# Where the tiles of a four-layer block lie in SBUF: weights at 448, halves and other 2 KB tiles at 128 modulo 512 bytes

## The chip, the core and the metric

The kernel runs on one NeuronCore of a Trainium2 chip. The metric is the device time of one execution, in microseconds: the median of the timed runs of the kernel before is 1500.3 us (1500.19 to 1500.99, three runs). The profiled execution, from which all rows come, took 1500.85 us.

## The reference

Two blocks follow one another on x of 256 positions by 1,024 features, all in float32. Cut to what matters for the work on the chip:

```python
def first_block(x, ...):                       # two layers
    for l in range(2):
        h = rms_norm(x, norm_mix[l])
        x = x + (pool_attn_mixer if l % 2 == 0 else rglru_mixer)(h, ...)
        h = rms_norm(x, norm_ffn[l])
        x = x + conv_ffn(h, ...)               # 1024 -> 2 x 2816 -> 1024

def hybrid_layer(x, pe, ...):                  # two layers of the second block
    proj = rms_norm(x, g_mix) @ w_in           # queries, keys, values, 3 x 1024 gates
    merged = (gates[0] * (o_mla @ w_branch[0]) + gates[1] * (o_diff @ w_branch[1])
              + gates[2] * (o_win @ w_branch[2]))
    x = x + merged @ w_out
    h = rms_norm(x, g_ffn)
    a = depthwise_conv(h @ w_ffn_gate, conv_w, conv_b)
    x = x + (gelu(a) * (h @ w_ffn_up)) @ w_ffn_down
    return x + sigmoid(rms_norm(x, g_ple_in) @ w_ple_gate) * rms_norm(pe @ w_ple_proj, g_ple)
```

Nearly all the arithmetic is products of x (or of something as wide) with weight matrices that are used once.

## The kernel before

The weights come from memory as one stream of chunks, each up to 128 partitions by 2,048 float32 (8 KB in a partition). `_push` (line 247) loads a chunk into `st`, ScalarE rounds it to `hi` (a float32r copy, line 262), and VectorE writes what the rounding lost to `lo` (line 263). There are three buffers of each, and two chunks are prepared ahead. Activations are kept as two halves in the same way: `xx` holds the normalised x transposed (both halves side by side, written at lines 391 and 392), `o` the outputs of the attention heads, `hg` the products inside the feed-forward nets, `w4` some others.

A product of two such pairs is three matmuls, `mm3` (line 277): high by high, high by low, low by high. TensorE multiplies a stationary operand (128 columns, loaded by a LDWEIGHTS of its own before every matmul) with a moving one of 256 to 512 columns. Two forms alternate:

- feature-major (`fm_pair`, `fm_first`, `fm_wide`, `gate`, `branch`): the weights are stationary, and the halves of x or of the attention move, 256 columns at a time (512 at line 608, where both halves of `xx` move at once);
- token-major (`tm_block`, `tm_wide`): the halves are stationary, and the weights move, 512 columns at a time.

```python
    def mm3(self, out, ah, al, bh, bl, start, stop):
        mm = self.pe.matmul
        mm(out, ah, bh, start=start, stop=False)
        mm(out, ah, bl, start=False, stop=False)
        mm(out, al, bh, start=False, stop=stop)
```

In a group of the profile `T<-xx,hi` means: written to PSUM tile `T`, moving operand `xx`, stationary operand `hi`; the first name behind the arrow is the moving one. Matmuls that go through the in-order wrapper show line 207.

The order of the work is set by a scheduler that the framework runs over the program as it is written; matmuls of the merge stage keep the written order. All weight chunks are issued on SyncE's queue.

A tile is asked for by a tag with `t` (line 227). All tiles of a tag share its buffers (`SB`, line 225, says how many), and a tag's buffers get their place in SBUF when it is asked for the first time, one tag behind the other in that order. So the order of first requests sets every address. A partition's row of a chunk, of `xx`, `o` and `hg` is cut in steps of multiples of 512 bytes: k blocks, halves and column blocks all start at the tile's own address modulo 512, except in one chunk of 416 columns for each hybrid layer.

Of the kernel before, what the change touches and what calls it, by code (L numbers as in the profile page):

```python
# [19 lines left out]
P = 128  # L20
S = 256
D = 1024
# [7 lines left out]
CHUNK = 2048  # L30
# [179 lines left out]
class Net:  # L210
# [66 lines left out]
# [5 lines that stand above are left out]
# [165 lines left out]
    def start(self):  # L447
        nc, ap = self.nc, self.ap
        self.vecs = self.t(list(ap["vec"].shape), "vec")
        self.ident = self.t([P, P], "ident")  # L450
        g0 = self.vat["gain0"]
        self.act_o.dma_start(self.ident, ap["ident"])
        self.act_o.dma_start(self.vecs[:, g0:g0 + KD], ap["vec"][:, g0:g0 + KD])
        self.x = self.t([P, 2, D], "x")
        self.sync_o.dma_start(self.x[:, 0, :], ap["x"][:P, :])
        for _ in range(3):
            self._push()
        self.rows = self.t(list(ap["row"].shape), "row")
        self.ones = self.t([P, P], "ones")
        self.sync_o.dma_start(self.vecs[:, g0 + KD:], ap["vec"][:, g0 + KD:])  # L460
        self.sync_o.dma_start(self.ones, ap["ones"])
        self.sync_o.dma_start(self.rows, ap["row"])
        self.acc = None
# [443 lines left out]
    def chained(self, mms):  # L907

        last = None
        for out, lhsT, rhs, start, stop in mms:  # L910
            ins = self.pe.matmul(out, lhsT, rhs, start=start, stop=stop)
            if last is not None:
                self.after(ins, [last])
            last = ins
# [506 lines left out]
```

## Time and profile before

| | |
|---|---|
| median of the runs | 1500.3 us (1500.19 to 1500.99) |
| profiled execution | 1500.85 us, its span 1499.0 us |
| PE (matmul) busy | 1486.7 us, 99% of the span |
| PEld (weight load) busy | 1328.7 us, 89% |
| DVE busy | 1160.4 us, 77% |
| ACT busy | 935.2 us, 62% |
| POOL busy | 108.0 us, 7% |
| DMA | 257.29 MB, 172 GB/s on average |

The busy time of PE is the union of its matmuls, which overlap; it says that one was always under way, not at which rate they follow one another. The rate is read from starts in the timeline, divided by the count between them.

### The profile page before, as it was taken

What the parts mean: (1) busy time and instruction counts of PE and PEld (TensorE: products, weight loads), DVE (VectorE), ACT (ScalarE), POOL (GpSimd) and SP (SyncE); (2) the same over time, 40 slices, a digit from 0 to 9 for tenths busy, and PEclk for the clock granted to TensorE, in tenths of its full rate; (3) what the DMA queues carried; (4) which work ended last, traced back from release to release, by engine and by line L of the source; (5) the groups of instructions that cost most, each with busy time, mean ns of one, the idle gap of its engine ahead of it and who ended that gap; (6) DMA issues with size and microseconds to landing.
All of it is one profiled execution on the core that took longest, in us unless ns stands there. A gap on an engine that the chain in (4) does not pass through costs nothing.

```text
span 1499.0 us, 24541 instructions
## 1 busy us (share of the span) xinstructions
PE 1486.7 (99%) x9540; PEld 1328.7 (89%) x9540; DVE 1160.4 (77%) x2257; ACT 935.2 (62%) x1684; POOL 108.0 (7%) x101
## 2 busy tenths in 40 slices
PE   8999999999999999999999999999999999999998
PEld 6789999999999998899988988888899998988896
DVE  6669777789797777885877877778886877877766
ACT  7757555586666556765765755656766664765554
POOL 0200000000000000012530000000003250000000
PEclk9999999999999999999999999999999999999999
DMA  7455455444454554543335455544443334555551
GB/s 285 160 190 197 170 197 193 165 148 169 158 208 171 195 175 159 197 169 113 136 119 190 171 206 186 197 169 167 168 183 126 130 125 169 190 197 178 190 194 56
DMA packets 37877, 257.29 MB, mean 172 GB/s; under 512 B 4385, under 2 KB 4769, under 8 KB 8321
## 3 DMA queue, kind: packets, MB, share of 16 engines
q1 hardware_dynamic: 36576, 252.38, 47.5%
q0 software_dynamic: 896, 3.28, 0.6%
q8 instruction: 75, 1.23, 0.3%
q14 instruction: 42, 0.34, 0.1%
q10 hardware_dynamic: 288, 0.07, 0.0%
HBM read 254.66 MB, written 1.05 MB: 171 GB/s over the span
## 4 chain that ended last, share of the span: by engine, by line
PE 95%; DVE 3%; issue 1%; ACT 1%; DMA 0%; SPq 0%; ACTq 0%
PE A L207 14%; PE A L279 10%; PE A L280 10%; PE A L281 10%; PE S L281 4%; PE S L280 4%; PE S L279 4%; PE T L281 4%; PE T L280 4%; PE T L279 4%; PE S L608 4%; PE T L608 4%; PE T L207 2%; PE S L207 2%; PE O L279 2%; PE O L280 2%
## 5 line engine op out<-in xcount | busy, mean ns | idle before, releaser
L263 DVE TENSOR_TENSOR lo<-st,hi 128x1024 fp32r<-128x1024 f32 (+3 forms) x480 | 574.2, 1210 | 143.1 <-ACT hi L262 142.1
L262 ACT ACTIVATE hi<-st 128x1024 fp32r<-128x1024 f32 (+3 forms) x480 | 490.0, 1043 | 245.3 <-PE A L207 65.6
L207 PE MATMUL A<-xx,hi 128*128 128x256 f32 x768 | 142.5, 287 | 0.0
L281 PE MATMUL S<-xx,lo 128*128 128x256 f32 x496 | 141.4, 285 | 0.0
L280 PE MATMUL S<-xx,hi 128*128 128x256 f32 x496 | 140.8, 284 | 0.0
L279 PE MATMUL S<-xx,hi 128*128 128x256 f32 x496 | 140.1, 283 | 0.0
L281 PE MATMUL T<-xx,lo 128*128 128x256 f32 x480 | 136.4, 284 | 0.0
L280 PE MATMUL T<-xx,hi 128*128 128x256 f32 x480 | 136.3, 284 | 0.0
L279 PE MATMUL T<-xx,hi 128*128 128x256 f32 x480 | 136.2, 284 | 0.0
L207 PEld LDWEIGHTS A<-xx,hi 128*128 128x128 f32 x768 | 118.2, 189 | 8.2 <-issue 7.9
L279 PE MATMUL A<-hi,xx 128*128 128x512 f32 (+2 forms) x304 | 117.1, 387 | 0.2 <-ACT xx L391 0.2
L280 PE MATMUL A<-lo,xx 128*128 128x512 f32 (+2 forms) x304 | 116.2, 382 | 0.0
L281 PE MATMUL A<-hi,xx 128*128 128x512 f32 (+2 forms) x304 | 115.9, 383 | 0.0
L281 PE MATMUL A<-hi,hg 128*128 128x512 f32 x294 | 115.1, 391 | 0.6 <-DVE hg L314 0.6
L279 PE MATMUL A<-hi,hg 128*128 128x512 f32 x294 | 115.6, 393 | 0.0
L280 PE MATMUL A<-lo,hg 128*128 128x512 f32 x294 | 115.4, 393 | 0.0
L207 PE MATMUL A<-xx,lo 128*128 128x256 f32 x384 | 108.3, 282 | 0.0
L1113 POOL TENSOR_SCALAR s<-s,at 128x256 f32<-128x256 f32 x56 | 56.4, 1024 | 577.5 <-DVE at L958 577.0
L279 PEld LDWEIGHTS S<-xx,hi 128*128 128x128 f32 x496 | 94.1, 190 | 0.1
L281 PEld LDWEIGHTS S<-xx,lo 128*128 128x128 f32 x496 | 93.8, 189 | 0.1
L280 PEld LDWEIGHTS S<-xx,hi 128*128 128x128 f32 x496 | 93.6, 189 | 0.1
L279 PEld LDWEIGHTS T<-xx,hi 128*128 128x128 f32 x480 | 91.1, 190 | 0.9
(377 smaller groups left out, 3464.2 us busy)
## 6 DMA issues: line engine op xcount, KB each, us to landing
st<-in_w_dram SPq DMA_DIRECT2D x230, 1024.0 KB, 4.8
st<-in_w_dram SPq DMA_DIRECT2D x4, 832.0 KB, 4.8
st<-in_w_dram SPq DMA_DIRECT2D x2, 768.0 KB, 4.2
x<-in_x_dram SPq DMA_DIRECT2D x2, 512.0 KB, 5.0
st<-in_w_dram SPq DMA_DIRECT2D x4, 256.0 KB, 6.5
st<-in_w_dram SPq DMA_DIRECT2D x2, 512.0 KB, 3.5
w<-in_gain_dram POOLq DMA_DIRECT2D x2, 512.0 KB, 4.0
out_dram<-x SPq DMA_DIRECT2D x4, 256.0 KB, 2.0
```

Source lines behind the costliest of these rows:

```text
L207: return lambda *a, **k: self.tc.keep_in_program_order(f(*a, **k))
L262: nc.scalar.activation(hi[:, c0:c1], st[:, c0:c1], AF.Copy)
L263: nc.vector.tensor_tensor(out=lo[:, c0:c1], in0=st[:, c0:c1], in1=hi[:, c0:c1].bitcast(F32), op=ALU.subtract)
L279: mm(out, ah, bh, start=start, stop=False)
L280: mm(out, ah, bl, start=False, stop=False)
L281: mm(out, al, bh, start=False, stop=stop)
L608: mm(banks[e], wh[:, k, c], self.xx[:, k, :], start=k == 0, stop=False)
L1113: nc.gpsimd.tensor_scalar(s[:, c], s[:, c], r[:, t:t + 1], None, op0=ALU.mult)
```

## The change

At the very start of the program, after `vec`, `ident` and `x`, one tile of each of 16 tags is asked for, in a chosen order, and never written. Nothing else is changed. The order, the number and the waits of the instructions on all five engines are the same in both programs, and so is the turn in which buffers of a tag are used; the lines behind move down by two.

```diff
         self.x = self.t([P, 2, D], "x")
+        for tag, n in (("st", CHUNK), ("hi", CHUNK), ("lo", CHUNK), ("ssx", 4), ("ess", 4), ("trcos", 32)) + (("xx", 4 * D), ("w4", D), ("o", D), ("hg", 512), ("w6", 1536), ("s", 512), ("pT", 512), ("qk", 512), ("w2", 512), ("bias", 512)):
+            self.t([P, n], tag)
         self.sync_o.dma_start(self.x[:, 0, :], ap["x"][:P, :])
```

The addresses in a partition that follow (first buffer of a tag, and what is left of it modulo 512), as the two programs place them:

| tag | holds | before | modulo 512 | after | modulo 512 |
|---|---|---|---|---|---|
| x, ident | x, identity | 19904, 19392 | 448 | the same | 448 |
| st, hi, lo | weight chunks | 28096, 52672, 77248 | 448 | the same | 448 |
| xx | halves of x, merged halves | 105024 | 64 | 102016 | 128 |
| w4 | projections, halves of the embedding | 131232 | 160 | 118400 | 128 |
| o | halves of the attention | 155808 | 160 | 142976 | 128 |
| hg | products of the nets, gates | 201344 | 128 | 159360 | 128 |
| w6 | queries, keys, merged sum | 189056 | 128 | 175744 | 128 |
| s | scores, net columns | 176288 | 160 | 188032 | 128 |
| pT | transposed probabilities, net columns | 184736 | 416 | 196224 | 128 |
| qk | transposed queries and keys, net columns | 172192 | 160 | 200320 | 128 |
| w2 | scratch | 121440 | 96 | 204416 | 128 |
| bias | position bias | 127136 | 160 | 208512 | 128 |
| ones | ones | 104512 | 64 | 215296 | 256 |
| rb | row scales | 217728 | 128 | 217888 | 288 |
| dist | distances | 218816 | 192 | 218976 | 352 |

The three small tags behind `lo` (`ssx`, `ess`, `trcos`) take 192 bytes, which lead from 448 to 128.

## Rows read from the trace of the kernel before

**Rows 1.** The page: TensorE's busy time, and the chain's shares by engine.
```profile
PE 1486.7 (99%) x9540; PEld 1328.7 (89%) x9540; DVE 1160.4 (77%) x2257; ACT 935.2 (62%) x1684; POOL 108.0 (7%) x101
...
PE 95%; DVE 3%; issue 1%; ACT 1%; DMA 0%; SPq 0%; ACTq 0%
```

**Rows 2.** Waits of PE: us in total, times, longest.
```profile
PE S L355 <- DMA ident<-in_ident_dram: 4.7, 1, 4.7
PE T L355 <- DMA x<-in_x_dram: 1.2, 1, 1.2
PE A L281 <- DVE hg L314: 0.6, 1, 0.6
PE A L279 <- ACT xx L391: 0.2, 1, 0.2
```

**Rows 3.** Windows: length, busy PE, PEld, DVE, ACT, POOL, clock, DMA share, GB/s.
```profile
243.60:260.63 17.03, 17.03 (x121) 16.03 (x120) 13.03 (x20) 9.50 (x15) 0.00 (x0) 1.00 0.53 188
854.18:870.93 16.75, 16.75 (x91) 14.36 (x90) 14.49 (x37) 9.87 (x16) 0.00 (x0) 1.00 0.55 194
```

**Rows 4.** Timeline of PE, one net unit: start, duration, group; first of each stream.
```profile
243.61 0.28 PE L279 MATMUL T<-xx,hi 128*128 128x256 f32 x1
...
255.12 0.39 PE L279 MATMUL A<-hi,hg 128*128 128x512 f32 x1
...
260.63 0.28 PE L279 MATMUL T<-xx,hi 128*128 128x256 f32 x1
```

**Rows 5.** Groups of PEld: count, busy us, mean ns.
```profile
L279 PEld LDWEIGHTS A<-hi,hg 128*128 128x128 f32 x294 | 55.3, 188 | 11.3
...
L207 PEld LDWEIGHTS A<-xx,hi 128*128 128x128 f32 x768 | 118.2, 189 | 8.2 <-issue 7.9
```

**Rows 6.** Timeline of PE, the product with w_out: its first, and the next's.
```profile
795.17 0.39 PE L279 MATMUL A<-hi,xx 128*128 128x512 f32 x1
...
817.47 0.49 PE L386 MATMUL S<-ident,x 128*128 128x128 f32 x3
```

**Rows 7.** Timeline of PE, 120 matmuls of the branches: first, and the next's.
```profile
1239.48 0.39 PE L207 MATMUL A<-o,hi 128*128 128x256 f32 x1
...
1253.78 0.39 PE L279 MATMUL A<-hi,xx 128*128 128x512 f32 x1
```

**Rows 8.** Timeline of PE, an earlier net unit's 96 matmuls.
```profile
141.58 0.28 PE L279 MATMUL T<-xx,hi 128*128 128x256 f32 x1
...
152.97 0.39 PE L279 MATMUL A<-hi,hg 128*128 128x512 f32 x1
```

**Rows 9.** Groups by form, halves stationary.
```profile
L279 PE MATMUL A<-hi,xx 128*128 128x512 f32 x240 | 96.5, 404 | 0.0
...
L281 PE MATMUL A<-hi,o 128*128 128x512 f32 x26 | 10.6, 406 | 0.0
...
L280 PE MATMUL T<-lo,xx 128*128 128x512 f32 x8 | 3.2, 395 | 0.0
```

**Rows 10.** Groups by form, halves moving.
```profile
L207 PE MATMUL A<-xx,hi 128*128 128x256 f32 x768 | 142.5, 287 | 0.0
...
L608 PE MATMUL S<-xx,hi 128*128 128x512 f32 x240 | 85.6, 394 | 0.0
...
L207 PE MATMUL A<-o,hi 128*128 128x256 f32 x256 | 47.3, 286 | 0.0
...
L281 PE MATMUL A<-xx,lo 128*128 128x256 f32 x112 | 31.3, 282 | 0.0
```

**Rows 11.** Timeline of PE, 32 wide pairs: the first, and the next stream's.
```profile
859.69 0.40 PE L608 MATMUL T<-xx,hi 128*128 128x512 f32 x1
...
870.92 0.40 PE L279 MATMUL A<-hi,hg 128*128 128x512 f32 x1
```

**Rows 12.** Groups by form of VectorE, the costliest.
```profile
L263 DVE TENSOR_TENSOR lo<-st,hi 128x1024 fp32r<-128x1024 f32 x460 | 557.1, 1224 | 131.6 <-ACT hi L262 130.7
```

## The prediction

> **What bounds the kernel now.** I read the engines' busy shares first, then the chain that ended last, then the waits, then the instruction groups, then single starts. The reader is to see that TensorE alone sets the time: its matmuls cover 99% of the span and the chain is 95% PE [rows 1]. All its waits that the profile names come to 6.7 us (4.7 + 1.2 + 0.6 + 0.2), most of it before the first matmul [rows 2]. So a buffer that comes free sooner, or a DMA that lands sooner, gives nothing; only a shorter step from one matmul to the next does. [...]
>
> The mean duration of a matmul in the groups (287 ns for 256 columns) is no price, since matmuls overlap. The price is the distance between starts. One unit of a feed-forward net before its wide form is 96 matmuls of 256 columns and 24 of 512. The 96 run from 243.61 to 255.12 us, 119.9 ns each; the 24 from 255.12 to 260.63 us, 229.6 ns each [rows 4]. [...] The weight loads take 188 to 189 ns each whatever tile they read [rows 5], and there is one for every matmul. [...]
>
> [...] Both of the following streams have 512 columns, moving from weight buffers at 448 modulo 512, with the same loop (`tm_wide`), and differ in where the stationary tile lies. With the nets' products (`hg`, at 128) it is 229.6 ns [rows 4]; with the merged halves in the x tile (`xx`, at 64), 96 matmuls from 795.17 to 817.47 us, 232.3 ns [rows 6]. So 128 is 2.7 ns better than 64 beside 448.
>
> For the moving operand there is one row only, and not of 128: 120 matmuls of 256 columns moving from `o` (at 160), with weights at 448 stationary, go from 1239.48 to 1253.78 us, 119.2 ns each [rows 7], against 119.9 for `xx` at 64. And the address isn't all: an earlier run of the same 96 matmuls at the same addresses takes 141.58 to 152.97 us, 118.6 ns each [rows 8]. Streams fall into one rhythm or another, 1.3 ns apart.
>
> [...]
>
> **The change part by part.** No instruction is added, removed or moved, on any queue, and no wait changes; tiles get other addresses. Weight buffers (`st`, `hi`, `lo`), `x` and `ident` keep theirs.
>
> 1. Stationary operand from 64 to 128, `xx` under 512 columns: 14 groups, of which the largest and the smallest are shown, 960 matmuls in all [rows 9]. At 2.7 ns: 2.6 us. All on the path, since PE waits for nothing between them.
> 2. Stationary operand from 160 to 128 (`o`, and the `w4` halves): 216 matmuls, the largest group of 26 shown [rows 9]. No clean stream of them stands in the trace; at the same 2.7 ns, 0.6 us. Bounds: nothing and twice that.
> 3. Moving operand from 64 to 128, `xx`, 256 columns: 13 groups, the largest and the smallest shown, 4,896 matmuls [rows 10]. This term decides, and its price is in no row. Upper end of the gain: what the stationary operand gives, 2.7 ns, if only the distance between the two operands counts: 13.2 us. Lower end: the same 2.7 ns lost, if the pair 128 moving, 448 stationary is a bad one; 13.2 us slower. The nearest row is `o` at 160, 0.7 ns better than 64, and the pair of 128 and 448 is the best that the trace shows, though with the roles exchanged. I take the middle of these two, 1.7 ns: 8.3 us.
> 4. Moving operand from 64 to 128, `xx`, 512 columns (L608): 480 matmuls [rows 10], at the same 1.7 ns: 0.8 us. With its partner of 256 columns such a pair takes 351 ns now (32 pairs from 859.69 to 870.92 us, [rows 11]).
> 5. Moving operand from 160 to 128 (`o` in the branches): 256 + 128 + 3 x 64 = 576 matmuls, the largest group shown [rows 10]. By terms 3 and the row of 160, 1.7 - 0.7 = 1.0 ns: 0.6 us; bounds 2 us either way.
> 6. VectorE, ScalarE and GpSimd tiles (`s`, `pT`, `qk`, `w2`, `bias` from 160, 416 or 96 to 128; `rb` from 128 to 288, `dist` from 192 to 352): I cost them at nothing. What hides them is TensorE: in the net's unit DVE is busy 13.03 us of 17.03 and ACT 9.50 [rows 3], so each could be 20% slower before it ended last. VectorE's largest group by far, 460 subtractions of 1,224 ns, reads `st` and `hi` and writes `lo`, none of which moves [rows 12]. Transposes read `ident` and their source in float32; they are few, and I leave them at nothing.
>
> Sum: 2.6 + 0.6 + 8.3 + 0.8 + 0.6 = 12.9 us of matmul steps. What is late next when they go? With 4 us of slack for DVE in a unit of 17 us that gets 0.15 us shorter, nothing; but a few waits behind norms don't shrink, so I count 12.5. The profiled execution took 1500.85 us (span 1499.0 and 1.85 around it), 0.5 above the median of 1500.3. 1500.85 - 12.5 = 1488.3, and against the median 1487.8. I say 1488.
>
> **The rivals.**
> *The weight load alone sees its address.* Then terms 1 and 2 stay and 3 to 5 vanish: 3.2 us, 1497.5. For it: the only clean pair of rows differs on the stationary side. Against it: `o` at 160 as moving operand is 0.7 ns faster than `xx` at 64, but that is less than the 1.3 ns between two rhythms of one address.
>
> *Nothing changes.* The difference between `hg` and `xx` comes from the rhythm or the position in the program, not from the address: 1500.5. For it: the two rhythms. Against it: 96 matmuls of `xx` and 24 of `hg` each keep their value where they recur. [...]
>
> *Slower: the distance has a sign.* In the stream of 229.6 ns the stationary operand lies 192 bytes past the moving one (128 - 448, modulo 512); in that of 232.3 ns it lies 128 past. After the change the 256-column matmuls have it 320 past (448 - 128), a distance no row shows; now it is 384. If 320 is a bad distance the 5,376 matmuls of terms 3 and 4 pay up to 2.7 ns, 14.5 us, less the 3.2 us won: 1500.5 + 11.3, about 1512. It decides from 0.6 ns a matmul on (3.2 / 5,376). For it: three in four of the matmuls whose operand moves are of this kind, and the trace has no row of that distance. Against it: 128, a multiple of 128 bytes, is the only placement in the trace that is better than the others.
>
> **How the numbers follow.** The forecast (both operands gain; its own range 1479 to 1493, from half the moving gain to 2.7 ns with the better rhythm's 1.3 ns on top) 0.52; the weight load alone 0.20; nothing 0.09; slower 0.19. About 0.2%, 3 us, can be told from no change. The second case, at 3.2 us, sits on that line: I give 0.13 of it to faster and 0.07 to same. Faster 0.65, same 0.16, slower 0.19. The range from 1478 to 1504 leaves out the far end of each side: the slow case beyond 1.2 ns a matmul, and gains above those two together.
>
> **What the profile after would show.** Right: the 96 matmuls of the net's unit below 118.6 ns a step, and `xx` under 512 columns at 229 to 230 ns, with `hg` unchanged at 229.6. Term 1 is wrong if the 96 of the merged halves still take 22.3 us. Term 3 is wrong if the unit's 96 still take 11.5 us, and the slow rival is right if they take over 11.6. Wrong for another reason: a wait of PE for DVE or ACT that grows beyond 1 us in sum, or busy times of VectorE's groups on `rb` or `s` that change by several per cent. The forecast as a whole fails if the step of the 256-column matmuls moves by less than 0.5 ns.

## The result, and the profile after

The changed kernel takes 1484.5 us (median of four runs, 1484.14 to 1485.4), against 1500.2 for the kernel before on the same chip (1499.89 to 1500.99): a ratio of 0.9895, 95% interval 0.9883 to 0.9907. The forecast was 1488.0, with a range of 1478 to 1504. The profiled execution took 1484.23 us, at a mean granted clock of 1.000 as before.

The page of the changed kernel, busy times and the chain's shares by engine:

```profile
span 1482.3 us, 24541 instructions
...
PE 1469.4 (99%) x9540; PEld 1312.3 (89%) x9540; DVE 1160.1 (78%) x2257; ACT 934.1 (63%) x1684; POOL 106.9 (7%) x101
...
PE 87%; DVE 8%; ACT 3%; issue 2%; DMA 0%; ACTq 0%
```

TensorE is busy for 17.3 us less, the other engines as long as before to within 1.1 us [rows 1]. More of the chain now passes through VectorE (8% against 3%), which invites the reading that PE waits for it. The waits of PE that the profile names (us in total, times, longest) say no; they are those of [rows 2]:

```profile
PE S L355 <- DMA ident<-in_ident_dram: 4.7, 1, 4.7
PE T L355 <- DMA x<-in_x_dram: 1.3, 1, 1.3
PE A L281 <- DVE hg L314: 0.6, 1, 0.6
PE A L279 <- ACT xx L391: 0.2, 1, 0.2
```

So the gain lies in the steps between matmuls: a step is the distance from the start of one matmul to the start of the next. PE's timeline of the net's unit (start, duration, group), whose fellow before is [rows 4]:

```profile
240.29 0.28 PE L279 MATMUL T<-xx,hi 128*128 128x256 f32 x1
...
251.60 0.40 PE L279 MATMUL A<-hi,hg 128*128 128x512 f32 x1
...
257.11 0.28 PE L279 MATMUL T<-xx,hi 128*128 128x256 f32 x1
```

The 96 matmuls of 256 columns step by 117.8 ns (11.31 us / 96), 2.1 less than before; the 24 of `hg` by 229.6, unchanged. The same timeline of the merged halves' 96 [rows 6], of the 32 wide pairs [rows 11], of a later unit's 96 and of the branches' 120 [rows 7], each with the start of what follows it:

```profile
785.27 0.39 PE L279 MATMUL A<-hi,xx 128*128 128x512 f32 x1
...
807.24 0.27 PE L386 MATMUL S<-ident,x 128*128 128x128 f32 x1
...
865.86 0.39 PE L610 MATMUL T<-xx,hi 128*128 128x512 f32 x1
...
877.17 0.39 PE L279 MATMUL A<-hi,hg 128*128 128x512 f32 x1
...
949.86 0.28 PE L279 MATMUL T<-xx,hi 128*128 128x256 f32 x1
...
960.77 0.39 PE L279 MATMUL A<-hi,hg 128*128 128x512 f32 x1
...
1225.01 0.39 PE L207 MATMUL A<-o,hi 128*128 128x256 f32 x1
...
1238.73 0.39 PE L279 MATMUL A<-hi,xx 128*128 128x512 f32 x1
```

Merged halves 228.9 ns (232.3 before); a wide pair 353.4 ns (351 before: slower); the later unit 113.6; the branches 114.3 (119.2 before).

For the whole program I added up the steps, by the kind of the matmul that starts them. A stream is a run of matmuls of one kind, a seam the place where one stream ends and the next begins. The number in brackets is the mean step in ns without the seams:

| matmuls | count | before: us (step) | after: us (step) | change, us |
|---|---|---|---|---|
| `xx` moving, 256 columns | 4,896 | 594.8 (119.4) | 581.7 (116.6) | -13.1 |
| `xx` stationary, 512 | 960 | 228.7 (232.5) | 224.7 (229.2) | -4.0 |
| `o`, `w4` stationary, 512 and 384 | 216 | 48.4 | 47.7 | -0.7 |
| `xx` moving, 512 (wide form) | 480 | 110.8 (230.7) | 112.8 (235.0) | +2.0 |
| `o` moving, 256 | 576 | 70.0 (118.3) | 68.0 (114.7) | -2.0 |
| `hg` stationary, 512 | 1,176 | 271.0 (229.5) | 270.9 (229.5) | -0.1 |
| float32 transposes | 504 | 59.1 | 60.3 | +1.2 |
| all matmuls | 9,540 | | | -16.7 |

The kinds not shown change by 0.1 us or less each. -16.7 us is the difference of the two spans (1499.0 and 1482.3); of it the medians show 15.7.

VectorE's largest group, by form (busy us, mean ns), is what it was [rows 12]:

```profile
L263 DVE TENSOR_TENSOR lo<-st,hi 128x1024 fp32r<-128x1024 f32 x460 | 557.6, 1225 | 125.3 <-ACT hi L262 124.8
```

### The profile page after: what moved, and what is told of

It is laid out like the page before. It is cut to its first block, busy times and chain, and to the rows that moved or that the text cites. A ratio compares the mean times of both kernels' runs of the same rounds, so it can differ in the third digit from the quotient of the medians.

```text
span 1482.3 us, 24541 instructions
## 1 busy us (share of the span) xinstructions
PE 1469.4 (99%) x9540; PEld 1312.3 (89%) x9540; DVE 1160.1 (78%) x2257; ACT 934.1 (63%) x1684; POOL 106.9 (7%) x101
## 4 chain that ended last, share of the span: by engine, by line
PE 87%; DVE 8%; ACT 3%; issue 2%; DMA 0%; ACTq 0%
PE A L207 11%; PE A L280 9%; PE A L279 9%; PE A L281 9%; PE S L279 4%; PE S L281 4%; PE S L280 4%; PE T L279 4%; PE T L281 4%; PE T L280 4%; PE S L610 4%; PE T L610 4%; DVE lo L263 3%; PE T L611 2%; PE S L611 2%
## 5 line engine op out<-in xcount | busy, mean ns | idle before, releaser
L262 ACT ACTIVATE hi<-st 128x1024 fp32r<-128x1024 f32 (+3 forms) x480 | 489.8, 1042 | 228.2 <-PE A L207 60.3
L207 PE MATMUL A<-xx,hi 128*128 128x256 f32 x768 | 138.8, 284 | 0.0
L207 PEld LDWEIGHTS A<-xx,hi 128*128 128x128 f32 x768 | 117.0, 188 | 8.2 <-issue 7.9
L281 PEld LDWEIGHTS T<-xx,lo 128*128 128x128 f32 x480 | 91.8, 191 | 0.0
```

The costliest lines, as they stand in the source:

```text
L207: return lambda *a, **k: self.tc.keep_in_program_order(f(*a, **k))
L262: nc.scalar.activation(hi[:, c0:c1], st[:, c0:c1], AF.Copy)
```

## The experiments

**How they are told.** All times are medians; the kernel before stood beside each on the same chip, and the ratios are to it. It took between 1500.2 and 1500.7 us each time, so the times of different runs can be set beside one another. Each trace is of one execution. Each edit is of the list of (tag, size in floats) that the change adds; a "pad" is a tile that nobody uses and moves what follows. Weights stay at 448 modulo 512 unless it is said. I write d for the address of the stationary operand less that of the moving one, modulo 256 (why 256, the sixth and seventh runs show). The change takes the 256-column matmuls of `xx` from d = 128 to 64, and the 512-column ones with `xx` stationary from 128 to 192.

The rows shown are PE's timeline (start in us, duration, group) of the run under whose number they stand: the first of a stream, and the first behind it.

**Theories.** A: alignment, both operands want a multiple of 128 bytes. B: the distance between the two operands counts. C: what counts are the other tiles that move along.

**1. Only `xx` back at 64, all else as after.**

```diff
- ("trcos", 32), ("xx", 4 * D), ("w4", D), ...
+ ("padx", 16), ("xx", 4 * D), ("padw", 16), ("w4", D), ...
```

> As the changed kernel, but the x tile (xx) alone goes back to 64 modulo 512; the attention halves, the nets' products and the rest stay at 128. Both theories that lay the gain on addresses (distance between the two operands, alignment of each operand) expect the streams of xx to go back: 96 matmuls of a net unit about 119.9 ns a step instead of 117.8, xx stationary under 512 columns 232.3 instead of 229.2, xx moving with 512 columns 230.7 instead of 235.0, and o moving to stay at 114.7: 4.0 + 13.1 - 2.0 = 15.1 us of the gain gone, about 1499 us. If the gain came from the other tiles or from the position of streams in the program, it stays near 1485.

1497.5 us (1497.17 to 1498.29), ratio 0.998 (0.997 to 0.9989). PE's timeline of the net's unit:

```profile
243.19 0.28 PE L279 MATMUL T<-xx,hi 128*128 128x256 f32 x1
...
254.71 0.40 PE L279 MATMUL A<-hi,hg 128*128 128x512 f32 x1
```

120.0 ns, as before. `xx` stationary is back at 232.5, the wide form at 230.6, and `o`, left at 128, keeps its 114.7. C falls for `xx`: 13 of the 16 us belong to its address alone; of the other 3, 2.7 are those of `o` and `w4` in the table above.

**2. Everything but `x` and `ident` shifted by 64 bytes, weights too (to 0; halves at 192).**

```diff
- (("st", CHUNK), ("hi", CHUNK), ...
+ (("pads", 16), ("st", CHUNK), ("hi", CHUNK), ...
```

> As the changed kernel, but weight buffers and halves are all 64 bytes further: weights at 0, halves at 192 modulo 512. The distance between any two operands is that of the changed kernel. Distance theory: the same streams, 1484.5 us within 2. Alignment theory (a tile that starts at a multiple of 128 is cheap to read): the halves lose it and the weights win it, so token-major streams go back to 232 to 233 ns (about +4 us) and the feature-major ones, whose stationary operand is now aligned, move by up to 3 ns either way: outside 1482 to 1487.

1484.0 us (1482.14 to 1484.64), ratio 0.9889 (0.9875 to 0.9904). The net's unit:

```profile
240.34 0.28 PE L279 MATMUL T<-xx,hi 128*128 128x256 f32 x1
...
251.64 0.40 PE L279 MATMUL A<-hi,hg 128*128 128x512 f32 x1
...
257.15 0.28 PE L279 MATMUL T<-xx,hi 128*128 128x256 f32 x1
```

117.7 and 229.6 ns, and over the whole program every kind as after: 116.4 (`xx` moving), 229.2 (`xx` stationary), 234.9 (wide), 114.7 ns (`o`). No shifted address is a multiple of 128 where it was one, and nothing is lost: A falls, B holds. (The weights gain the alignment that the halves lose. That one aligned operand of the two would be enough is ruled out by the third run, where the halves are aligned and the gain is gone.)

**3. Halves at 256.**

```diff
- ("trcos", 32), ("xx", 4 * D), ...
+ ("trcos", 32), ("padx", 32), ("xx", 4 * D), ...
```

> As the changed kernel, but the halves and the other 2 KB tiles lie at 256 modulo 512, weights at 448. Alignment theory (multiples of 128): as the changed kernel, 1484.5 within 2. Distance theory with a sign: feature-major matmuls now have the stationary operand 192 past the moving one, the distance of the good token-major stream, and token-major ones 320 past; the two forms exchange their lot, so the 96 of a net unit fall below 117 ns or hg leaves 229.5 by over 1 ns. Distance without a sign: 192 either way, as the changed kernel.

1497.8 us (1497.03 to 1498.3), ratio 0.9982 (0.9972 to 0.9991). The net's unit:

```profile
242.94 0.28 PE L279 MATMUL T<-xx,hi 128*128 128x256 f32 x1
...
254.24 0.39 PE L279 MATMUL A<-hi,hg 128*128 128x512 f32 x1
...
259.84 0.28 PE L279 MATMUL T<-xx,hi 128*128 128x256 f32 x1
```

117.7 ns for 256 columns but 233.3 for `hg`, which took 229.6 at d = 192 and now has d = 64. Modulo 256, 192 is -64, so the operands are as far apart as before, the other way round: the distance has a sign. Against the changed kernel the 256-column matmuls of `xx`, now at d = 192, lose 5.4 us (117.7 ns over all of them), `hg` 4.5 and `xx` stationary 4.3.

The trace settles another thing. In each hybrid layer 48 matmuls have 256 columns of the weights moving over `xx`, the roles exchanged. They took 113.5 ns here (d = 64), 117.8 in the changed kernel (192), 118.5 in the kernel before (128) and 119.9 in the fourth run (0): with 256 columns the price goes with d, whichever of the two tiles moves.

**4. Halves at 448, the weights' own residue (d = 0).**

```diff
- ("ssx", 4), ("ess", 4), ("trcos", 32), ("xx", 4 * D), ...
+ ("xx", 4 * D), ...
```

> As the changed kernel, but the halves and the other 2 KB tiles lie at 448 modulo 512, as the weights do: distance 0. Distance theory: the operands start in step, the worst case if reads of one stretch of the 512 bytes get in each other's way: hg over 232 ns, a net unit's 96 over 119.9, over 1500 us. Alignment theory: as a start at 64 modulo 128, like the kernel before: about 1500 to 1504, since hg loses too (1,176 x 3 ns = 3.5 us). No address effect: 1485.

1498.5 us (1498.18 to 1499.27), ratio 0.9987 (0.9978 to 0.9996). PE's timeline of the net's unit in this run:

```profile
241.92 0.28 PE L279 MATMUL T<-xx,hi 128*128 128x256 f32 x1
...
253.43 0.40 PE L279 MATMUL A<-hi,hg 128*128 128x512 f32 x1
...
258.90 0.28 PE L279 MATMUL T<-xx,hi 128*128 128x256 f32 x1
```

A miss for `hg`, 227.9 ns where I expected over 232, and for the total, where each theory that counts on addresses said 1500 or more. d = 0 is the best distance for 512 columns moving from the weights, and the worst for 256 columns moving from the halves (119.5 to 119.7 over all of them, against 119.1 to 119.4 at d = 128). That called for `hg` alone at 448.

**5. `hg` alone at 448.**

```diff
- ("o", D), ("hg", 512), ("w6", 1536), ..., ("bias", 512)
+ ("o", D), ("w6", 1536), ..., ("bias", 512), ("padh", 80), ("hg", 512)
```

> As the changed kernel, but the nets' products (hg) lie at 448 modulo 512, where the weights lie: distance 0 for hg alone. Distance theory, by the stream of distance 0 seen in the run with everything at 448: hg 228.0 ns a step instead of 229.5, 1,176 x 1.5 = 1.7 us, all other streams as in the changed kernel: about 1482.8. If what counts there was that all tiles lay at 448, or hg's own start, no change: 1484.5.

1483.9 us (1483.54 to 1484.51), ratio 0.989 (0.9875 to 0.9905). `hg` gained its 2.3 us (227.2 ns), and `xx` moving lost 2.5, though no address of its own had changed. One of the places is the late unit, whose 96 matmuls took 113.6 ns a step in the changed kernel (949.86 to 960.77, above); its timeline in this run:

```profile
949.03 0.28 PE L279 MATMUL T<-xx,hi 128*128 128x256 f32 x1
...
960.33 0.39 PE L279 MATMUL A<-hi,hg 128*128 128x512 f32 x1
```

117.7 ns. So at d = 64 these matmuls have two steps, some 113.5 and 117.8 ns, and hold either for a whole stream. I call them the fast and the slow rhythm. What else moved has a say in which: `hg`, whose streams come ahead of these, or the other tiles that its new place in the list shifts. (Each of the two rhythms shows in some of the 256-column streams at d = 192 too: 113.3 to 113.7 ns in 7 of the third run's 70 streams of `xx` with 24 or more matmuls.)

**6 and 7. Other residues: `xx` at 192 and `hg` at 384; `xx` and `hg` at 320.** `o` is at 0 and at 384.

```diff
- ("trcos", 32), ("xx", 4 * D), ("w4", D), ("o", D), ("hg", 512), ..., ("bias", 512)
+ ("trcos", 32), ("padx", 16), ("xx", 4 * D), ("w4", D), ("pado", 80), ("o", D), ..., ("padh", 96), ("hg", 512)    # 6
+ ("trcos", 32), ("padx", 48), ("xx", 4 * D), ("w4", D), ("pado", 16), ("o", D), ..., ("padh", 112), ("hg", 512)   # 7
```

> Halves of x at 192, of the attention at 0, nets' products at 384 modulo 512; weights stay at 448. Distances not seen so far: 256 for x either way, 448 and 64 for the attention, 448 for hg. Distance theory: where both forms have the same distance (256) the matmul of 256 columns costs the same whichever operand moves, within 0.5 ns (x moving over the weights, and the weights moving over x in the chunk of the window's keys); its value has no row yet. Alignment theory: x at 192 is as x at 64, 119.4, and hg at 384 as hg at 128, 229.5. Total between 1480 and 1502.

> Halves of x at 320, of the attention at 384, nets' products at 320 modulo 512; weights stay at 448. Distance theory names the prices from rows of other kernels: stationary minus moving is 128 for x moving, seen in the kernel before with the roles exchanged (weights moving 256 columns over x at 64: 118.5 ns), so x moving 118.5; it is 384 for x and hg stationary under 512 columns, seen in the kernel before in x moving 512 columns: 230.7, so 230.7 for both. Alignment theory: x at 320 as x at 64, 119.4 moving and 232.5 stationary, hg 232.5. Total by the distances about 5,376 x 2 ns above the changed kernel: 1494 to 1498.

1498.9 us (ratio 0.999, 0.9981 to 1.0) and 1499.3 (0.9993, 0.9983 to 1.0003). The merged halves' 96 in the sixth and in the seventh run:

```profile
794.00 0.39 PE L279 MATMUL A<-hi,xx 128*128 128x512 f32 x1
...
815.79 0.27 PE L386 MATMUL S<-ident,x 128*128 128x128 f32 x1
```

```profile
793.36 0.39 PE L279 MATMUL A<-hi,xx 128*128 128x512 f32 x1
...
815.66 0.27 PE L386 MATMUL S<-ident,x 128*128 128x128 f32 x1
```

227.0 and 232.3 ns: 192 gives what 448 gave in the fourth run (227.4 over all), and 320 what 64 gave in the kernel before. Expected for the seventh were 230.7, with a period of 512, and a total of 1494 to 1498; both are misses. What was expected of the sixth came: 256 columns cost the same whichever operand moves (119.5 ns with `xx` moving, 119.9 with the weights). Each stream of `xx` repeats after 256 bytes, as do `o` at 384 (114.7, as at 128), `o` at 0 (117.8, as at 256: 117.1) and `hg` at 384 (229.1, as at 128).

**8. The changed kernel without the wide form** (by the table above, a wide pair loses from the change).

```diff
- self.ffn(gi, body, aside, True)
+ self.ffn(gi, body, aside)
```

> As the changed kernel, but the feed-forward nets of the second block never use the wide form: three matmuls of 256 columns in place of one of 512 and one of 256, 480 times. In the changed kernel such a pair takes 235.0 + 118.4 = 353.4 ns. Streams of 256 columns run in one of two rhythms there, 117.8 and 113.3 ns. If the slow rhythm holds in these nets, 3 x 117.8 = 353.4: no change, 1484.5. If the fast one holds, 339.9: 6.5 us faster, 1478. In the kernel before the same edit would have cost 3 x 119.9 - 351.1 = 8.6 ns each, 4.1 us.

1487.3 us (1486.3 to 1488.59), ratio 0.9913 (0.9898 to 0.9928): slower than after, outside what I expected (1478 to 1484.5). 5,856 matmuls of 256 columns now take 696.1 us, where 4,896 and the 480 wide ones took 694.5, because the late unit, which never had the wide form, has gone over to the slow rhythm here too, as its timeline shows:

```profile
949.78 0.28 PE L279 MATMUL T<-xx,hi 128*128 128x256 f32 x1
...
961.09 0.40 PE L279 MATMUL A<-hi,hg 128*128 128x512 f32 x1
```

117.8 ns. In the slow rhythm the two forms cost the same: three matmuls of 256 columns take 3 x 117.8 = 353.4 ns, and a wide pair takes 353.4.

**9. `hg` at 480 (d = 32, bad for `hg` itself).** The list of the fifth run with another pad:

```diff
- ("padh", 80), ("hg", 512)
+ ("padh", 88), ("hg", 512)
```

> As the changed kernel, but the nets' products (hg) lie at 480 modulo 512: distance 32 to the weights, not seen so far for a stationary operand. Distance theory modulo 256: hg alone changes, anywhere between the 227.2 ns of distance 0 and the 233.4 of distance 64, 1482 to 1489 us, and all streams of x and o keep their prices unless the rhythm of the 256-column streams behind hg changes. The rival, that a neighbour of the seam sets the rhythm: hg's place decides whether the nets' 96 run at 117.8 or 113.3 ns a step, up to 4,333 x 4.5 ns = 19 us faster or, where the fast runs of now are lost, 2.5 us slower.

1479.8 us (1479.16 to 1480.47), ratio 0.9862 (0.9845 to 0.9878). The net's unit in PE's timeline of this run:

```profile
238.10 0.28 PE L279 MATMUL T<-xx,hi 128*128 128x256 f32 x1
...
248.99 0.39 PE L279 MATMUL A<-hi,hg 128*128 128x512 f32 x1
...
254.59 0.28 PE L279 MATMUL T<-xx,hi 128*128 128x256 f32 x1
```

`hg` pays, 233.3 ns a step and 5.0 us in all; but the nets' 96 run at 113.4, in every unit, and `xx` moving wins 9.6 us over the changed kernel. All that differs from the fifth run is that `hg`, and the small tiles placed behind it, lie 32 bytes further; `xx`, `o` and the weights stay where they were.

**10. `xx` at 96, `hg` at 288, `o` at 224.**

```diff
- ("trcos", 32), ("xx", 4 * D), ("w4", D), ("o", D), ("hg", 512), ..., ("bias", 512)
+ ("padx", 24), ("xx", 4 * D), ("w4", D), ("pado", 32), ("o", D), ..., ("padh", 16), ("hg", 512)
```

> Halves of x at 96, of the attention at 224, nets' products at 288 modulo 512; weights stay at 448. With the weights stationary the distances are 352 (96 modulo 256) for x and 224 for o, the two next to those already seen; with the weights moving, 160 for x, 32 for o, 96 for hg. Alignment theory: starts at odd multiples of 32 bytes are the worst, all streams above the kernel before. Distance theory modulo 256 asks only that the prices lie near their neighbours': x moving between 114.7 (64) and 119.4 (128), hg between 232.5 and 233.4, o moving between 117.7 (192) and 119.6 (0); total 1488 to 1502.

1499.0 us (1498.07 to 1499.79), ratio 0.9991 (0.9981 to 1.0): `xx` moving 118.2 ns, `xx` stationary 233.5, `hg` 234.0. It fills the table of d below. `hg` (expected between 232.5 and 233.4) and `o` (117.0, expected between 117.7 and 119.6) fall outside the prices of the distances next to theirs, so one can't read a price off its neighbours. For 512 columns moving from the weights no odd multiple of 32 was good (233.1 to 234.0 ns); whether the distance does that, or that these halves start at no multiple of 64 bytes, no run tells apart.

**11. The ninth run without the wide form.**

```diff
+ ..., ("padh", 88), ("hg", 512)
- self.ffn(gi, body, aside, True)
+ self.ffn(gi, body, aside)
```

> The nets' products at 480 modulo 512 and x at 128, as in the run e9_hg480, and the wide form replaced by three matmuls of 256 columns, as in e8_narrow. Seam theory (what a token-major stream of hg leaves behind sets the rhythm of the 256-column stream after it, and hg at 480 leaves the fast one): all nets of the second block run at 113.5 ns a step; 480 times 3 x 113.5 = 340.5 instead of 234.7 + 118.3 = 353.0: 6.0 us below e9_hg480, 1473.8. If the fast rhythm in e9_hg480 was tied to the stages before, and the second block's nets fall into the slow one as they did in e8_narrow: 353.4 each and the late nets' 113.6 lost, 1480 to 1482.

1474.6 us (1473.36 to 1475.58), ratio 0.9826 (0.9813 to 0.984): 9.9 us better than the change, the fastest of all. Its late unit in PE's timeline:

```profile
957.96 0.28 PE L279 MATMUL T<-xx,hi 128*128 128x256 f32 x1
...
968.85 0.39 PE L279 MATMUL A<-hi,hg 128*128 128x512 f32 x1
```

113.4 ns. 5,856 matmuls of 256 columns take 679.3 us, 16.8 less than in the eighth run. Once the fast rhythm holds, the narrow form beats the wide one: three matmuls of 256 columns, 3 x 113.4 = 340 ns, stand for a wide pair of 353.

**12. The same with `hg` at 320 (d = 128).**

```diff
- ..., ("padh", 88), ("hg", 512)
+ ..., ("padh", 48), ("hg", 512)
```

> As e11_hg480_narrow, but the nets' products lie at 320 modulo 512: distance 128 to the weights, whose price under 512 columns is 232.5 ns (nets' products in e7_scan_b, x in the kernel before) against 233.2 at 480. If the rhythm is fast behind every token-major stream that isn't at 229.5 or 227.2 ns, the streams of 256 columns keep 113.5 and 1,176 x 0.7 = 0.8 us are won: 1473. If it depends on more than that, the nets' streams go back to 117.8 in part or whole: up to 4,333 + 1,440 matmuls x 4.3 ns = 25 us more.

1477.0 us (1475.83 to 1477.73), ratio 0.9842 (0.9829 to 0.9856). That is 2.4 us slower than the eleventh, where 0.8 us faster was expected if the rhythm held. Its rhythms lie between those of the ninth and the fifth: the nets' 96 behind a stream of `hg` run at 113.4 ns, but the longer run ahead of a net's first such stream is fast in one net out of four. PE's timeline of two nets of the second block, 144 matmuls each from the second chunk on:

```profile
823.15 0.28 PE L279 MATMUL S<-xx,hi 128*128 128x256 f32 x1
...
839.47 0.39 PE L279 MATMUL A<-hi,hg 128*128 128x512 f32 x1
...
1274.54 0.28 PE L279 MATMUL S<-xx,hi 128*128 128x256 f32 x1
...
1291.50 0.39 PE L279 MATMUL A<-hi,hg 128*128 128x512 f32 x1
```

113.3 and 117.8 ns, with the same instructions ahead and the same addresses modulo 512. So these alone don't settle the rhythm. Whole addresses may: each of `st`, `hi` and `lo` has three buffers, used in turn, and each hybrid layer takes 73 chunks, one more than 24 full turns, so these two nets meet the weights in buffers that stand one place of the turn apart. The three nets whose longer run is slow all begin at the same place of the turn, the fast one at another. The weight buffer isn't the whole of it either, since in the first net the slow run (117.8 ns) reads all three buffers and the fast 96 behind it (113.4 ns) read two of the same.

## Why the prediction was right, and where its sizes were off

**The mechanism held.** PE sets the time, none of its waits that the profile names grew by more than 0.1 us, and the step from one matmul to the next depends on where the two operands lie. The first run shows it for `xx` alone (120.0 ns in the net's unit at 64, 117.8 at 128). Of the signs named ahead, all that stood for the forecast came: the unit's 96 below 118.6 (117.8), `xx` stationary at 229 to 230 (229.2), `hg` unchanged, VectorE's groups unchanged.

**Term 1** (2.6 us) measured 4.0: the step fell by 3.3 ns rather than 2.7 (3.2 us), and some 0.8 us came in at seams. **Term 2** (0.6) measured 0.7.

**Term 3** decided, and was mis-sized: 8.3 us predicted, 13.1 measured, the upper end that was worked out for it. The middle, 1.7 ns a step, was chosen by the row of `o` at 160, as though 160 lay on the way from 64 to 128. It doesn't: 448 - 160 is 32 modulo 256, a distance that none of the other 256-column matmuls has (118.3 ns over all that move from `o`). And the 2.8 ns are not one number: in the first block's nets the step went to 117.8, in the late units to 113.6, so the mean mixes two rhythms at one address. The prediction had seen two rhythms (118.6 and 119.9), and allowed 1.3 ns for them, where 4.3 lie between the two after. That this term has the right sign is luck in part: no row had d = 64, and the reason given for 128 bytes fell in the second run.

**Term 4** had the wrong sign: a gain of 0.8 us predicted, a loss of 2.0 measured. The price of the 256-column form was carried over to 512 columns; d = 64 is the best distance tried for the one (114.1 to 117.1 ns in the mean; elsewhere 117.0 at the least), and one of the two worst for the other (235.0).

**Term 5** (0.6) measured 2.0, for the same reason as term 3. **Term 6** was nothing, as said, but for 1.2 us at the float32 transposes. These steps belong to the waits that don't shrink, for which the prediction took off 0.4 us, and they follow the speed of the streams ahead: with `xx` back at 64 (first run) they take 59.2 us, nearly as before, and among them those that read `s` take 20.7 us, against 21.5 in the changed kernel and 20.8 before. In two places, 0.7 us of the 1.2, PE now comes early enough to wait for ScalarE, which the list of waits doesn't show because the records of the two matmuls nearly meet (in the place shown here the fifth transpose lasts to 651.90 us). The changed kernel, then the kernel before:

```profile
650.21 1.71 ACT L965 ACTIVATE s<-s,at 128x256 f32<-128x256 f32 x4 [0.93 <-DVE at L960]
...
651.97 0.33 PE L207 MATMUL T<-ident,s 128*128 128x128 f32 x1
```

```profile
657.16 1.71 ACT L963 ACTIVATE s<-s,at 128x256 f32<-128x256 f32 x4 [0.43 <-DVE at L958]
...
658.83 0.60 PE L207 MATMUL T<-ident,s 128*128 128x128 f32 x4
```

ScalarE is done with `s` at 651.92 us, and the sixth transpose starts at 651.97, 401 ns behind the fifth; before, they followed one another at 109 ns.

**"Bounds and nothing late next"** held. The slack in a unit covered VectorE, and the chain's 8% for DVE cost PE nothing that its waits show; what is late next shows only at the transposes just named.

**The rivals.** *The weight load alone sees its address* (1497.5): terms 3 and 5 are 15.1 of the 16.7 us, so it falls. *Nothing changes* (1500.5): the same instructions in the same order took 1484.5 us against 1500.2, 1.1% less with addresses alone, so it falls too. *The distance has a sign* was right as a mechanism (third run) and wrong in its value: 320, that is 64 modulo 256, is a good distance for 256 columns (116.6 ns for `xx` moving, against 119.4 at 128). My argument against it, that 128 is a better placement because it is a multiple of 128 bytes, fell in the second run. The prediction came out well while one of its reasons was wrong.

**What stays open.** What repeats every 256 bytes, and why the step goes with the distance of the two operands at all; distances finer than 32 bytes (not tried); and what puts a stream into one rhythm or the other. Moving `hg`, and the tiles behind it, turns it (fifth and ninth run), so it isn't the distance of the two operands alone; the last run shows both at the same addresses modulo 512 with the same instructions ahead, but not at the same weight buffers.

## What to carry to other kernels

Where TensorE is busy for the whole span with short matmuls that each load their own weights, put the step between starts, by form, beside the distance of the two operands' addresses; pads of some dozens of bytes ahead of a tile moved the time here by about one per cent (1.1 in the change, 1.4 in the ninth run). Choose by distance and not by alignment, and separately for each number of columns, since d = 0 was the best for 512 columns moving from the weights (227.2 to 228.0 ns) and among the worst for 256 (119.5 to 119.7). A tile's move can change the rhythm of a neighbouring stream, which weighed more in the ninth run (9.6 us won) than the tile's own streams (5.0 lost), so measure the whole program.

## What the runs showed of the hardware

Not expected were the dependence on the distance modulo 256 bytes, with other good distances for 512 columns than for 256, and two rhythms 4.3 ns apart at one distance. Mean steps in ns over all matmuls of a kind and run (d as defined above: stationary less moving; float32r, one weight load of 128 columns each, clock 1.00); at d = 64 the two rhythms of single streams stand in the second column, the means there being 114.1 to 117.1:

| d | 512 columns moving from the weights | 256 columns moving from `xx` or `o` | 512 columns moving from `xx` (wide) |
|---|---|---|---|
| 0 | 227.2 to 228.0 | 119.5 to 119.7 | 236.1 to 236.3 |
| 32 | 233.2 | 118.3 | not tried |
| 64 | 233.3 | 113.5 or 117.8 | 235.0 |
| 96 | 234.0 | 118.2 | 229.4 |
| 128 | 232.5 | 119.1 to 119.4 | 230.7 |
| 160 | 233.5 | not tried (119.9 with the weights moving) | not tried |
| 192 | 229.1 to 229.9 | 117.1 to 117.8 | 232.2 |
| 224 | 233.1 | 117.0 | not tried |

In the wide form each matmul of 512 columns is followed by one of 256, so the third column is no clean comparison of the roles.
